# The linear attention's projections and decays first, two blocks' decays at once, softmax attention between its states

## The chip, the cores and the metric

The kernel runs on one core of a Trainium2 chip. The metric is device time in microseconds (us) for one launch. TensorE (PE in the profile) does the matrix products, VectorE (DVE) the elementwise and reducing work, ScalarE (ACT) the functions and most evictions of the matmul accumulators, GpSimd (POOL) and SyncE (SP) mostly issue transfers. Each engine executes its own list of instructions strictly in the order in which the program put them; an instruction that waits holds up everything behind it on its engine.

## What is computed

One decoder block for 512 tokens of width 1024, cut here to what matters:

```python
mod = silu(c) @ w_ada + b_ada                     # shift1, scale1, gate1, shift2, scale2, gate2
h = rms_norm(x, norm1_w) * (1 + scale1) + shift1
aq, ak, av, gq, gk, gv, gg, glr = split(h @ w_in)  # 512,128,128,256,256,512,512,16 columns
att = sliding_window_attention(aq, ak, av, sinks)  # 8 heads, 2 kv heads, window 128
log_a = log_sigmoid(glr @ gate_up + gate_bias) / 16
go = gla_chunked(gq, gk, gv, log_a)                # 4 heads: a decayed running state over the sequence
go = rms_norm(go, gla_norm_w) * silu(gg)
x = x + gate1 * (concat(att, go) @ w_out)
h2 = rms_norm(x, norm2_w) * (1 + scale2) + shift2
x = x + gate2 * peer_ffn(h2, wq, subkeys, u, v)    # product-key retrieval over 16384 experts
return rms_norm(x, final_norm_w)
```

In the linear attention, with b the running sum of log_a inside a block, the weight between a query at time t and a key at s <= t is sum over d of q[t,d] k[s,d] exp(b[t,d] - b[s,d]); the inner sum over earlier blocks is carried in a state S that is multiplied by exp(b_last) and gains k exp(b_last - b) times v.

## The kernel before

The tokens lie in four blocks of 128 (n = 0 to 3). The program has a **front**, all of the block up to the second norm, and then the expert part (queries against the keys, a dense product with u, routing, gathers). Only the front is touched by the change. Its steps:

- **mod_part(v)** makes one sixth of `mod` for all 1024 columns: the weights come as four 1 MB transfers (`wa`), and VectorE multiplies and adds eight 128x1024 slices into `macc` (L163, L165). Parts 0 and 1 are done in halves by `mod_half` (L228); `modT` (L234) then gives the scale and shift of the norm, and `h`, `hTh`, `hTl` (L257 to L261) are the normed, transposed tokens split into a high and a low part.
- **Projections.** `w_in` comes in nine groups of 256 columns, each a 1 MB transfer (`wi`). Groups 0 and 1 are the attention's queries, 2 its keys and values, 3 and 4 the linear attention's queries `gq` and keys `gk`, 5 and 6 its values `gv`, 7 and 8 its output gate `gg`. Each group is split into two halves of high and low parts (ScalarE L59, VectorE L60), and each product is three matmuls, high-high, low-high, high-low (L64 to L66). `proj_T` (groups 0 to 4) gives a transposed result in matmuls of 512 columns, `proj_N` (5 to 8) a plain one in matmuls of 256 columns.
- **attention(n)**: twice four heads: scores `sc` into the two-bank accumulator (L333), scaled and masked (L335), row maximum (L341), exponentials with row sums on ScalarE (L345), division (L351), transposes `pt` (L360) evicted by ScalarE to `PT` (L361), products with the values `po` (L366), eviction to `mixA` (L369).
- **decays**: `glr`, then `z`, `e`, and `la` (L375 to L394), from log_sigmoid.
- **gla_prep(n)**, for one block: the running sum `b` (L428), and for seven levels (halves of 64, 32, ..., 1 tokens) the difference to the middle of each group, the later half one way (L438), the earlier the other (L437), so that all exponents are negative; one exponential over all of E (L441); the late halves times q, the early halves times k (L445, L446).
- **gla_scores(n)**: matmuls of E with itself give each level's scores `pa` (L473, L478), in the same two-bank accumulator that the attention's scores use (one buffer), and VectorE copies each level's part into `at` under a mask (L481, L486).
- **gla_state(n)**: `go` from the state and from `at` (L496, L497), the state's update (L501 to L512), the norm of `go` into `gv` (L517 to L521).
- **gla_gate(n)**: gate times normed output (L526, L527), transposes `gt` (L530), high and low parts `gh`, `gl`, `ah`, `al` (L534 to L541).
- **mixers(n0)** for two blocks at a time: the product with `w_out` (`pw`, weights `wo`), `mg` and the residual `x` (L602, L603), the second norm `xn` (L611), transposes `x2t` (L620), `h` (L623), `h2Th`, `h2Tl` (L625, L626).

Weights that are to be split wait in a ring of three raw 1 MB buffers, shared by `wi` and `wa`; a transfer into a buffer starts when the last reader of its old content is done. The program's text gives the steps an order of importance; a scheduler turns it into the fixed list of each engine from its own estimate of the times, so a small change in the text moves instructions on all engines.

Order of the steps in the text before: projections 0, 1, 2; attention 0 to 3; decays; projection 3; mod 2; projection 4; masks; prep and scores 0; projections 5, 6; prep and scores 1; state 0; projection 7; mod 3; state 1; prep and scores 2; projection 8; mod 4; the silu of `gg`; gates 0 and 1; state 2; prep and scores 3; state 3; mixers of blocks 0, 1; gates 2 and 3; mixers of blocks 2, 3.

Of the kernel before, what the change touches and what calls it, by code (L numbers as in the profile page):

```python
# [41 lines left out]
def peer_block_kernel(ctx: ExitStack, tc: tile.TileContext, a: dict, out: bass.AP):  # L42
# [202 lines left out]
    for half in range(2):  # L245
        mod_half(1, half)
        if half == 1:
            fetch(a["w_in"][1], 1, 256, "wi")
        mod_half(0, half)
        if half == 0:  # L250
            fetch(a["w_in"][0], 0, 256, "wi")
        else:
            x_transposes(range(4, KD))
        for k in range(4 * half, 4 * half + 4):
# [6 lines left out]
            nc.vector.tensor_tensor(hTl[:, k, :], h32, hTh[:, k, :], OP.subtract)  # L261
# [39 lines left out]

    proj_T(0, (qT[:, 0, :], qT[:, 1, :]))
    proj_T(1, (qT[:, 2, :], qT[:, 3, :]), bank)
    vT = frA.tile([P, T], F32, tag="h32", bufs=4, name="vT")
    proj_T(2, (kT, vT))
    pv = bank("pv")
    for n in range(NT):
        nc.tensor.transpose(pv[:, n * P:(n + 1) * P], vT[:, n * P:(n + 1) * P], ident)
    nc.scalar.activation(vN.rearrange("p a b -> p (a b)"), pv, AF.Copy)


    am = frT.tile([P, 256], F32, name="am")
    nc.vector.memset(am, 0.0)
    nc.gpsimd.affine_select(am[:, :P], am[:, :P], pattern=[[1, P]], compare_op=OP.is_gt, fill=NEG,
                            base=0, channel_multiplier=-1)
    nc.gpsimd.affine_select(am[:, P:], am[:, P:], pattern=[[-1, P]], compare_op=OP.is_ge, fill=NEG,
                            base=0, channel_multiplier=1)
# [57 lines left out]
    wg = raw([P, KD, 16], "wglr")  # L375
    nc.sync.dma_start(wg, a["w_glr"])
    wgh, wgl = hilo(wg, [P, KD, 16], "wglr", nc.vector)
    pg = pbank("pglr")
    for k in range(KD):
        mm3(pg[:16, :], wgh[:, k, :], wgl[:, k, :], hTh[:, k, :], hTl[:, k, :], k == 0, k == KD - 1)  # L380
    nc.scalar.activation(glrT, pg[:16, :], AF.Copy)

    for j in range(2):
        pz = bank(f"pz{j}")
        nc.tensor.matmul(pz, gup[:, j * P:(j + 1) * P], glrT, start=True, stop=True)
        z = frA.tile([P, T], F32, tag="h32", bufs=4, name=f"z{j}")
        e = frA.tile([P, T], F32, tag="h32", bufs=4, name=f"e{j}")
        nc.scalar.activation(z, pz, AF.Identity, bias=gbT[:, j:j + 1])
        nc.scalar.activation(e, z, AF.Abs)
        nc.scalar.activation(e, e, AF.Exp, scale=-1.0)  # L390
        nc.scalar.activation(e, e, AF.Ln, bias=1.0)
        for n in range(NT):
            tsl = slice(n * P, (n + 1) * P)
            nc.vector.scalar_tensor_tensor(la[n][:, j, :], z[:, tsl], 0.0, e[:, tsl], op0=OP.min, op1=OP.subtract)  # L394
    proj_T(3, [[t[:, j, :] for t in gq] for j in range(2)])
    mod_part(2, frA, "m4", 2, dst=gate1b)
    proj_T(4, [[t[:, j, :] for t in gk] for j in range(2)])


    lm = frG.tile([P, NL + 1, P], BF, name="lm")  # L400
    ia = frA.tile([P, P], I32, tag="h32", bufs=4, name="ia")
    ib = frA.tile([P, P], I32, tag="h32", bufs=4, name="ib")
    nc.gpsimd.iota(ia, pattern=[[1, P]], base=0, channel_multiplier=0)
    nc.gpsimd.iota(ib, pattern=[[0, P]], base=0, channel_multiplier=1)
    xf = frA.tile([P, P], F32, name="xf")
    nc.vector.tensor_tensor(ia, ia, ib, OP.bitwise_xor)
    nc.vector.tensor_copy(xf, ia)
    nc.vector.tensor_scalar(lm[:, NL, :], iop, 0.0, None, op0=OP.is_gt)
    nc.vector.tensor_tensor(xf, xf, lm[:, NL, :], OP.mult)
    for L in range(NL):  # L410
        m = 64 >> L
        nc.vector.tensor_scalar(lm[:, L, :], xf, float(m), None, op0=OP.is_ge)
        nc.vector.scalar_tensor_tensor(lm[:, L, :], xf, float(2 * m), lm[:, L, :], op0=OP.is_lt, op1=OP.mult)
    nc.vector.tensor_copy(lm[:, NL, :], ident)
    sm = frG.tile([P, 256], F32, name="sm")
    nc.vector.memset(sm, 1.0)
    nc.vector.memset(sm.rearrange("p (a b) -> p a b", a=2)[:, :, 0:1], 0.0)
    S = [frG.tile([P, 2, P], F32, name=f"S{j}") for j in range(2)]
    for t in S:
        nc.gpsimd.memset(t, 0.0)  # L420

    def gla_prep(n, pool):
        b = pool.tile([P, 256], F32, tag="b", bufs=1, name=f"b{n}")
        q = pool.tile([P, 256], F32, tag="q", bufs=1, name=f"q{n}")
        k = pool.tile([P, 256], F32, tag="k", bufs=1, name=f"k{n}")
        v2 = lambda t: t.rearrange("p (j t) -> p j t", j=2)
        nc.vector.tensor_scalar(v2(b), la[n], 1.0 / TAU, None, op0=OP.mult)
        nc.vector.tensor_tensor_scan(b, sm, b, 0.0, op0=OP.mult, op1=OP.add)  # L428
        nc.vector.tensor_scalar(v2(q), gq[n], 0.125, None, op0=OP.mult)
        nc.vector.tensor_copy(v2(k), gk[n])  # L430
        E = pool.tile([P, NL + 2, 256], F32, tag="E", bufs=1, name=f"E{n}")
        half = lambda t, m: t.rearrange("p (g w) -> p g w", w=2 * m)
# [668 lines left out]
```

## Time and profile before

| what | value |
|---|---|
| time, median of 3 runs | 1595.04 us (1592.78 to 1595.13) |
| profiled execution | 1595.75 us, span 1594.0 us, mean granted TensorE clock 0.975 |
| TensorE / VectorE / ScalarE busy | 94% / 80% / 42% of the span |
| first matmul of the expert queries (`pq`), the end of the front | 319.03 us after the span's start |
| last matmul of the last projection (`pn`) | starts 190.15 us |
| last matmul with `w_out` (`pw`) | starts 291.76 us |

Rows of a timeline are: start (us), duration (us), engine, line, operation, result<-sources, shape, count, and in brackets how long the engine had been idle before it and whose event ended that wait. Rows of a group are: line, engine, operation, names, shapes, count | busy us, mean ns of one | idle us before them and its releasers. Rows of windows are: from:to, length, then for each engine the busy time (and the instructions), then the granted TensorE clock (1.00 is full), the transfer engines' share and GB/s. Durations in one engine's list can overlap a little: an instruction is fed while the one before it drains.

### The profile page before, as it was taken

How to read it: one execution, taken by the hardware profiler on the slowest of the kernel's cores; microseconds unless marked ns; L12 is line 12 of the kernel's file. 1: busy time of each engine (PE TensorE's matmuls, PEld its weight loads, DVE VectorE, ACT ScalarE, POOL GpSimd, SP SyncE). 2: the span in 40 equal slices, each digit the busy share in tenths (PEclk: the TensorE clock that was granted, in tenths of full speed). 3: DMA queues.
4: the chain of work that ended last, by engine and by line, in shares of the span. 5: the costliest groups of instructions: out<-in, count | busy, mean ns of one | idle time of the engine just before them, and what ended most of it. 6: DMA issues, size and time to landing. Idle time of an engine off the chain costs nothing.

```text
span 1594.0 us, 23349 instructions
## 1 busy us (share of the span) xinstructions
PE 1504.8 (94%) x8787; PEld 1339.3 (84%) x8787; DVE 1282.2 (80%) x2613; ACT 675.1 (42%) x1071; POOL 415.9 (26%) x323
## 2 busy tenths in 40 slices
PE   4999976699999999999899999999999999999997
PEld 3779865598898999999888888888888888888885
DVE  7587886459997899798578888878888788788987
ACT  5364533533344656665333333333333333333333
POOL 0000000034430000003233434434434444343550
PEclk9999978799999999999999999999999999999998
DMA  9525423335244767579988988989898998898893
GB/s 346 179 100 183 153 80 128 110 106 211 88 161 140 221 205 243 181 226 315 413 336 314 361 320 328 347 324 374 319 337 342 336 362 324 328 345 330 298 329 137
DMA packets 154928, 409.60 MB, mean 257 GB/s; under 512 B 10288, under 2 KB 77120, under 8 KB 142400
## 3 DMA queue, kind: packets, MB, share of 16 engines
q1 hardware_dynamic: 108736, 261.30, 46.5%
q0 software_dynamic: 36864, 134.23, 22.8%
q10 hardware_dynamic: 9216, 12.59, 2.1%
q8 instruction: 68, 1.11, 0.3%
q14 instruction: 44, 0.36, 0.1%
HBM read 366.14 MB, written 41.94 MB: 256 GB/s over the span
## 4 chain that ended last, share of the span: by engine, by line
PE 59%; DVE 5%; DMA 3%; ACT 1%; issue 1%; DVEq 0%; ACTq 0%
PE acc L65 11%; PE acc L64 11%; PE acc L66 11%; PE ph L66 8%; PE ph L64 8%; PE ph L65 8%; PE pg L824 3%; DVE o L817 1%; DMA u<-in_uT_dram 1%; DVE o L812 1%; DMA gr<-Gd 1%; DMA gu<-in_u_dram,ix_u 1%; ACT gs L826 0%; DVE oh L769 0%; DVE oh L767 0%
## 5 line engine op out<-in xcount | busy, mean ns | idle before, releaser
L837 POOL DMA_INDIRECT gu<-in_u_dram,ix_u x128 | 175.4, 1370 | 535.4 <-DVE o L817 275.2
L847 POOL DMA_INDIRECT gv<-in_vP_dram,ix_v x128 | 168.0, 1313 | 215.3 <-DVE gu L839 184.3
L852 DVE SCALAR_TENSOR_TENSOR gacc<-gv,hg,gacc 128x1024 f32<-128x1024 f32 x127 | 162.6, 1280 | 4.1 <-DMA gv<-in_vP_dram,ix_v 4.0
L839 DVE SCALAR_TENSOR_TENSOR gu<-gu,h2n 128x1024 f32<-128x1024 f32 x128 | 156.0, 1219 | 5.6 <-DMA gu<-in_u_dram,ix_u 5.6
L981 ACT ACTIVATE Ah<-ge 128x384 fp32r<-128x384 f32 x64 | 33.6, 525 | 155.5 <-PE acc L65 155.5
L981 ACT ACTIVATE Ah<-gel 128x384 fp32r<-128x384 f32 x64 | 33.6, 525 | 154.4 <-PE acc L65 154.4
L826 ACT ACTIVATE gs<-pg 128x512 f32<-128x512 f32 x96 | 94.3, 1104 | 9.9 <-PE pg L824 9.9
L817 DVE TENSOR_TENSOR o<-o,gp 128x1024 bf16<-128x1024 bf16 x144 | 91.0, 687 | 4.3
L824 PE MATMUL pg<-o,o 128*128 128x128 bf16 x1152 | 79.3, 223 | 5.8 <-DVE o L817 5.7
L824 PEld LDWEIGHTS <-o 128*128 128x128 bf16 x1152 | 69.3, 99 | 15.2 <-issue 8.4
L982 DVE TENSOR_TENSOR Al<-gel,Ah 128x384 fp32r<-128x384 f32 x64 | 35.6, 556 | 45.3 <-ACT Ah L981 45.3
L650 ACT ACTIVATE ge<-ph 128x384 f32<-128x384 f32 x128 | 60.7, 474 | 26.5 <-PE ph L66 26.4
L812 DVE TENSOR_TENSOR o<-iot,t 128x2048 bf16<-128x2048 bf16 x48 | 58.5, 1219 | 7.5 <-ACT t L792 7.5
L60 POOL TENSOR_TENSOR uc0l<-u,uc0h 128x1024 fp32r<-128x1024 f32 x1 | 2.8, 2838 | 197.4 <-ACT uc0h L59 197.4
L982 DVE TENSOR_TENSOR Al<-ge,Ah 128x384 fp32r<-128x384 f32 x64 | 35.5, 555 | 18.9 <-ACT Ah L981 18.7
L977 DVE TENSOR_TENSOR ge<-ge,gr 128x384 f32<-128x384 f32 x64 | 35.4, 553 | 13.5 <-ACT ge L650 13.5
L165 DVE SCALAR_TENSOR_TENSOR macc<-wa,scs,macc 128x1024 f32<-128x1024 f32 x28 | 39.9, 1425 | 6.6 <-DMA wa<-in_w_ada_dram 6.3
L977 DVE TENSOR_TENSOR gel<-gel,gr 128x384 f32<-128x384 f32 x64 | 32.8, 553 | 0.4 <-DMA gel<-gsp 0.4
L718 DVE MAX8 TVa<-scm 128x8 f32<-128x128 f32 x64 | 15.6, 306 | 18.8 <-ACT scm L710 18.8
L64 PE MATMUL pq<-h2Th,wq_0h 128*128 128x512 f32 (+1 forms) x80 | 29.4, 367 | 0.8 <-ACT h2n L633 0.8
L65 PE MATMUL pq<-h2Tl,wq_0h 128*128 128x512 f32 (+1 forms) x80 | 28.4, 355 | 0.0
L66 PE MATMUL pq<-h2Th,wq_0l 128*128 128x512 f32 (+1 forms) x80 | 28.3, 353 | 0.0
(2587 smaller groups left out, 5151.8 us busy)
## 6 DMA issues: line engine op xcount, KB each, us to landing
u<-in_uT_dram SPq DMA_DIRECT2D x64, 1024.0 KB, 8.4
v<-in_vP_dram SPq DMA_DIRECT2D x64, 1024.0 KB, 8.2
Gd<-gs SPq DMA_DIRECT2D x24, 1024.0 KB, 5.9
gr<-Gd SPq DMA_DIRECT2D x16, 1536.0 KB, 8.3
wa<-in_w_ada_dram SPq DMA_DIRECT2D x20, 1024.0 KB, 5.8
gsp<-ge ACTq DMA_DIRECT2D x64, 192.0 KB, 3.6
gel<-gsp SPq DMA_DIRECT2D x32, 384.0 KB, 6.5
wi<-in_w_in_dram SPq DMA_DIRECT2D x9, 1024.0 KB, 5.0
```

Source lines behind the costliest of these rows:

```text
L64: nc.tensor.matmul(acc, lh, rh, start=start, stop=False)
L65: nc.tensor.matmul(acc, lh, rl, start=False, stop=False)
L66: nc.tensor.matmul(acc, ll, rh, start=False, stop=stop)
L812: nc.vector.tensor_tensor(o12.rearrange("p g s k r -> p (g s) k r"), iot[:, None].to_broadcast([P, 2 * H, P, 2]), t12[:, g0:g0 + H].rearra ...
L817: nc.vector.tensor_tensor(o2[:, :, m], o12[:, :, 1], gp3[:, g0:g0 + H, m, None].to_broadcast([P, H, P, 2]), OP.mult)
L824: nc.tensor.matmul(pt[:, i, :], o12[:, g, 0, :, r], o2[:, g, m, :, r], start=(m == 0), stop=(m == 2))
L826: nc.scalar.activation(gs[:, :, t0 + 4 * f:t0 + 4 * f + 4].rearrange("p b a -> p a b"), pt, AF.Copy)
L837: nc.gpsimd.indirect_dma_start(out=ur, out_offset=None, in_=a["u"], in_offset=bass.IndirectOffsetOnAxis(ap=ix_u[:, s:s + 1], axis=0))
L839: nc.vector.scalar_tensor_tensor(ur, ur, 1.0, h2n, op0=OP.mult, op1=OP.mult, accum_out=hid[:, s:s + 1])
L847: nc.gpsimd.indirect_dma_start(out=vr, out_offset=None, in_=a["vP"], in_offset=bass.IndirectOffsetOnAxis(ap=ix_v[:, s:s + 1], axis=0))
L852: nc.vector.scalar_tensor_tensor(gacc, vr, hg[:, s:s + 1], gacc, op0=OP.mult, op1=OP.add)
L982: nc.vector.tensor_tensor(Al, gef, Ah, OP.subtract)
```

## The change

Only the front changes, in these ways.

1. **Order of the text**: projection 3, decays, projection 4, projection 0, mod 2, prep of blocks 0 and 1, projection 1, scores 0, projection 2, attention 0, scores 1, projection 5, attention 1, prep of blocks 2 and 3, projection 6, state 0, attention 2, scores 2, state 1, projection 7, attention 3, scores 3, projection 8, silu, state 2, state 3, mod 3, mod 4, then gates 0 to 3, mixers of blocks 0, 1, mixers of blocks 2, 3. The groups fetched ahead are 3 and 4, not 0 and 1.
2. **Prep for two blocks at once**, 512 columns wide: one subtraction a level (all with the same sign), then the absolute value on ScalarE and one exponential with the scale -1/16. The division by 16 and the factor 0.125 of `gq` move into that scale and into the eviction of projection 3; the copies of `q` and `k` go away.
3. **One E for both preps**, which later holds the gate: `gg[n]` is the n-th slice of E. The evictions of projections 7 and 8 therefore come after the reads of E by scores 2 and 3.
4. **Gate**: `gg` is multiplied by the norm weight for all blocks after the silu; blocks 2 and 3 take the gate in the instruction that norms `go`. `ah` is made in one instruction instead of two, `al` too.
5. Masks, states and the eight `at` tiles (four before) are set up at the very start; `wg` has buffers of its own; the pool `gp` of the expert part is allocated later.

The scheduler's lists show where this puts the instructions. Three places follow.

**VectorE around the norm's end**, where `hTl`, the low part of the normed tokens, is made (names: `macc_308`/`macc_355` the last half part of mod 1 or 0, `macc_1056`/`macc_650` the sums of mod 2, `wa_0`, `wa_2` its 1 MB pieces). Before:

```order
L228 SCALAR_TENSOR_TENSOR macc_308<-mixA_126,scs,macc_308 128x512
L234 TENSOR_TENSOR modT<-mt,vec 128x4
L259 TENSOR_SCALAR h_7_358<-xt_341,aT,modT 128x512
L261 TENSOR_TENSOR hTl<-h_4_346,hTh 128x512
L261 TENSOR_TENSOR hTl<-h_7_358,hTh 128x512
```

After:

```order
L267 SCALAR_TENSOR_TENSOR macc_355<-mixA_117,scs,macc_355 128x512
L202 TENSOR_SCALAR macc_650<-wa_0_651,scs 128x1024
L204 SCALAR_TENSOR_TENSOR macc_650<-wa_0_651,scs,macc_650 128x1024
L273 TENSOR_TENSOR modT<-mt,vec 128x4
L298 TENSOR_SCALAR h_7_405<-xt_388,aT,modT 128x512
L204 SCALAR_TENSOR_TENSOR macc_650<-wa_2_655,scs,macc_650 128x1024 x2
L300 TENSOR_TENSOR hTl<-h_4_393,hTh 128x512
L300 TENSOR_TENSOR hTl<-h_7_405,hTh 128x512
```

Four instructions of mod 2 now stand ahead of `hTl`.

**TensorE in the attention's middle** (`sc` scores, `pt` transposes, `po` products with values, `pj` and `pn` projections, `mt` the column sums of mod 3 and 4, `gb` those of mod 2). Before, with projection matmuls above and below:

```order
L66 MATMUL pj_1027<-hTh,wi_1l 128x512
L333 MATMUL sc_688<-kT,qT 128x256 x3
L366 MATMUL po_562<-PT_589,vN 64x128 x4
L360 MATMUL pt_627<-ident,sS_600 128x128 x4
L333 MATMUL sc_688<-kT,qT 128x256
L172 MATMUL gb_1075<-macc_1056,ones 128x512
L366 MATMUL po_562<-PT_626,vN 64x128 x4
L333 MATMUL sc_738<-kT,qT 128x256 x4
L64 MATMUL pj_1091<-hTh,wi_0h 128x512
```

After, from the last matmul of projection 6 (the next projection matmul, of projection 7, stands 30 rows further on):

```order
L66 MATMUL pn_1681<-wi_1h,hTl 128x256
L384 MATMUL sc_1190<-kT,qT 128x256 x4
L384 MATMUL sc_1425<-kT,qT 128x256 x4
L216 MATMUL mt_2096<-ones,macc_2079 128x1 x8
L411 MATMUL pt_1168<-ident,sS_1141 128x128 x4
L417 MATMUL po_1140<-PT_1167,vN 64x128 x4
L411 MATMUL pt_1179<-ident,sS_1141 128x128 x4
L417 MATMUL po_1140<-PT_1178,vN 64x128 x4
L411 MATMUL pt_1216<-ident,sS_1189 128x128 x4
L384 MATMUL sc_1473<-kT,qT 128x256 x4
```

In the 30 rows between projections 6 and 7 there are attention 1 and 2, scores 2, state 0 and the column sums, and no projection.

**VectorE in that same stretch** has the sums of mod 4 (`macc_2106`) between the attention's steps:

```order
L204 SCALAR_TENSOR_TENSOR macc_2106<-wa_2_2111,scs,macc_2106 128x1024
L402 TENSOR_SCALAR sS_1189<-sS_1189,Z_1198 128x256 x4
L204 SCALAR_TENSOR_TENSOR macc_2106<-wa_2_2111,scs,macc_2106 128x1024
L386 SCALAR_TENSOR_TENSOR sS_1424<-sc_1425,am 128x1024
L204 SCALAR_TENSOR_TENSOR macc_2106<-wa_4_2115,scs,macc_2106 128x1024
L392 TENSOR_REDUCE mx_1431<-sS_1424 128x4
```

Before, these sums stood among the projections' and the later states' instructions. The diff, cut to its core (mod_part, mixers and the expert part keep their text):

```diff
-    for n in range(NT):
+    for i in range(2):
         for nm, lst in (("la", la), ("gq", gq), ("gk", gk)):
-            lst.append(frG.tile([P, 2, P], F32, tag="blk", bufs=3 * NT, name=f"{nm}{n}"))
+            lst.append(frG.tile([P, 2, 2, P], F32, tag="blk", bufs=6, name=f"{nm}{i}"))
-    gg = [frG.tile([P, 512], F32, tag="gg", bufs=NT, name=f"gg{n}") for n in range(NT)]
+    Eg = frG.tile([P, NL + 2, 512], F32, name="Eg")
+    gg = [Eg[:, n, :] for n in range(NT)]
...
-            fetch(a["w_in"][1], 1, 256, "wi")
+            fetch(a["w_in"][4], 4, 256, "wi")
...
-            fetch(a["w_in"][0], 0, 256, "wi")
+            fetch(a["w_in"][3], 3, 256, "wi")
...
-    for n in range(NT):
-        attention(n)
...
+    def gla_prep(i):
+        flat = lambda t: t.rearrange("p n j t -> p (n j t)")
+        q, k = flat(gq[i]), flat(gk[i])
+        b = frG.tile([P, 512], F32, tag="b", bufs=1, name=f"b{i}")
+        for n in range(2):
+            c2 = slice(n * 256, (n + 1) * 256)
+            nc.vector.tensor_tensor_scan(b[:, c2], sm, flat(la[i])[:, c2], 0.0, op0=OP.mult, op1=OP.add)
+        E = Eg
...
         for L in range(NL):
             m = 64 >> L
-            bv, ev = half(b, m), half(E[:, L, :], m)
-            ref = bv[:, :, m - 1:m].to_broadcast([P, 128 // m, m])
-            nc.vector.tensor_tensor(ev[:, :, :m], ref, bv[:, :, :m], OP.subtract)
-            nc.vector.tensor_tensor(ev[:, :, m:], bv[:, :, m:], ref, OP.subtract)
...
+            bv = grp(b, 2 * m)
+            nc.vector.tensor_tensor(grp(E[:, L, :], 2 * m), bv, bv[:, :, m - 1:m].to_broadcast([P, 256 // m, 2 * m]),
+                                    OP.subtract)
...
-        nc.scalar.activation(E, E, AF.Exp)
...
+        nc.scalar.activation(E[:, :NL, :], E[:, :NL, :], AF.Abs)
+        nc.scalar.activation(E[:, :NL + 1, :], E[:, :NL + 1, :], AF.Exp, scale=-1.0 / TAU)
+        nc.scalar.activation(E[:, NL + 1, :], b, AF.Exp, scale=1.0 / TAU)
...
+            if gated:
+                nc.vector.scalar_tensor_tensor(gv[n][:, gsl], go[:, gsl], r4[:, h:h + 1], gg[n][:, gsl], op0=OP.mult,
+                                               op1=OP.mult)
+            else:
+                nc.vector.tensor_scalar(gv[n][:, gsl], go[:, gsl], r4[:, h:h + 1], None, op0=OP.mult)
...
+    proj_T(3, [[t[:, :, j, :] for t in gq] for j in range(2)], scale=0.125)
+    decays()
+    proj_T(4, [[t[:, :, j, :] for t in gk] for j in range(2)], bank)
+    proj_T(0, (qT[:, 0, :], qT[:, 1, :]))
+    mod_part(2, frA, "m4", 2, dst=gate1b)
+    gla_prep(0)
+    proj_T(1, (qT[:, 2, :], qT[:, 3, :]), bank)
+    gla_scores(0)
...
+    attention(0)
+    gla_scores(1)
     proj_N(5, gv, 0)
+    attention(1)
+    gla_prep(1)
     proj_N(6, gv, 256)
-    gla_ahead(1)
-    gla_state(0, *ats[0])
+    gla_state(0, False)
+    attention(2)
+    gla_scores(2)
+    gla_state(1, False)
     proj_N(7, gg, 0)
-    mod_part(3, frA, "m4", 2)
-    gla_state(1, *ats[1])
-    gla_ahead(2)
+    attention(3)
+    gla_scores(3)
     proj_N(8, gg, 256)
-    mod_part(4, frA, "m4", 2)
     for t in gg:
         nc.scalar.activation(t, t, AF.Silu)
...
+    gla_state(2, True)
+    gla_state(3, True)
+    mod_part(3, frA, "m4", 2)
+    mod_part(4, frA, "m4", 2)
...
-    for n in (0, 1):
+    for n in range(NT):
         gla_gate(n)
-    gla_state(2, *ats[2])
-    gla_ahead(3)
-    gla_state(3, *ats[3])
-    mixers(0)
-    for n in (2, 3):
-        gla_gate(n)
-    mixers(2)
+    for n in range(0, NT, 2):
+        mixers(n)
```

More of the change, by code (lines that the diff above doesn't have):

```diff
@@ L147, in peer_block_kernel @@
     gup = frA.tile([16, 256], F32, name="gup")
+    am = frT.tile([P, 256], F32, name="am")
+    nc.vector.memset(am, 0.0)
+    nc.gpsimd.affine_select(am[:, :P], am[:, :P], pattern=[[1, P]], compare_op=OP.is_gt, fill=NEG,
+                            base=0, channel_multiplier=-1)
+    nc.gpsimd.affine_select(am[:, P:], am[:, P:], pattern=[[-1, P]], compare_op=OP.is_ge, fill=NEG,
+                            base=0, channel_multiplier=1)
+    lm = frG.tile([P, NL + 1, P], BF, name="lm")
+    ia = frA.tile([P, P], I32, tag="h32", bufs=4, name="ia")
+    ib = frA.tile([P, P], I32, tag="h32", bufs=4, name="ib")
+    nc.gpsimd.iota(ia, pattern=[[1, P]], base=0, channel_multiplier=0)
+    nc.gpsimd.iota(ib, pattern=[[0, P]], base=0, channel_multiplier=1)
+    xf = frA.tile([P, P], F32, name="xf")
+    nc.vector.tensor_tensor(ia, ia, ib, OP.bitwise_xor)
+    nc.vector.tensor_copy(xf, ia)
+    nc.vector.tensor_scalar(lm[:, NL, :], iop, 0.0, None, op0=OP.is_gt)
+    nc.vector.tensor_tensor(xf, xf, lm[:, NL, :], OP.mult)
+    for L in range(NL):
+        m = 64 >> L
+        nc.vector.tensor_scalar(lm[:, L, :], xf, float(m), None, op0=OP.is_ge)
+        nc.vector.scalar_tensor_tensor(lm[:, L, :], xf, float(2 * m), lm[:, L, :], op0=OP.is_lt, op1=OP.mult)
+    nc.vector.tensor_copy(lm[:, NL, :], ident)
+    sm = frG.tile([P, 256], F32, name="sm")
+    nc.vector.memset(sm, 1.0)
+    nc.vector.memset(sm.rearrange("p (a b) -> p a b", a=2)[:, :, 0:1], 0.0)
+    S = [frG.tile([P, 2, P], F32, name=f"S{j}") for j in range(2)]
+    for t in S:
+        nc.gpsimd.memset(t, 0.0)
+    atz = [frG.tile([P, 2, P], F32, name=f"at{i}") for i in range(8)]
+    for t in atz:
+        nc.gpsimd.memset(t, 0.0)
     nc.scalar.activation(scs, cT, AF.Exp, scale=-1.0)
@@ L300, in proj_N, with decays @@
                 nc.scalar.activation(dst[n + s][:, col:col + 256], pt[:, s, :], AF.Copy)
[L302 to L317, printed above, removed]
+    def decays():
+        pg = pbank("pglr")
+        for k in range(KD):
+            mm3(pg[:16, :], wgh[:, k, :], wgl[:, k, :], hTh[:, k, :], hTl[:, k, :], k == 0, k == KD - 1)
+        nc.scalar.activation(glrT, pg[:16, :], AF.Copy)
+        for j in range(2):
+            pz = bank(f"pz{j}", ("pt", "po")[j])
+            nc.tensor.matmul(pz, gup[:, j * P:(j + 1) * P], glrT, start=True, stop=True)
+            z = frA.tile([P, T], F32, tag="h32", bufs=4, name=f"z{j}")
+            e = frA.tile([P, T], F32, tag="h32", bufs=4, name=f"e{j}")
+            nc.scalar.activation(z, pz, AF.Identity, bias=gbT[:, j:j + 1])
+            nc.scalar.activation(e, z, AF.Abs)
+            nc.scalar.activation(e, e, AF.Exp, scale=-1.0)
+            nc.scalar.activation(e, e, AF.Ln, bias=1.0)
+            for i in range(2):
+                tsl = slice(i * 256, (i + 1) * 256)
+                two = lambda t: t[:, tsl].rearrange("p (n t) -> p n t", n=2)
+                nc.vector.scalar_tensor_tensor(la[i][:, :, j, :], two(z), 0.0, two(e), op0=OP.min, op1=OP.subtract)
     def attention(n):
@@ L369, in attention @@
         nc.scalar.activation(mixA[n].rearrange("p a b -> p (a b)"), po, AF.Copy)
-    for n in range(NT):
-        attention(n)
[L375 to L432, printed above, removed]
+    def gla_prep(i):
[6 more added lines that the diff above has]
+        E = Eg
+        grp = lambda t, w: t.rearrange("p (g w) -> p g w", w=w)
@@ L462, in gla_scores @@
+    preps = {}
+    def gla_scores(n):
+        q, k, E = preps[n // 2][:3]
+        off = n % 2 * 256
         U16 = mybir.dt.uint16
@@ L495, in gla_state @@
             if n > 0:
-                nc.tensor.matmul(go[:, gsl], qe[:, j * P:(j + 1) * P], S[j][:, s, :], start=True, stop=False)
+                nc.tensor.matmul(go[:, gsl], qe[:, off + j * P:off + (j + 1) * P], S[j][:, s, :], start=True, stop=False)
             nc.tensor.matmul(go[:, gsl], at[j][:, s], gv[n][:, gsl], start=(n == 0), stop=True)
@@ L867, in peer_block_kernel @@
     gather_to.n = 0
-    for n in (0, 1):
+    for n in range(NT):
         gla_gate(n)
-    gla_state(2, *ats[2])
-    gla_ahead(3)
-    gla_state(3, *ats[3])
-    mixers(0)
-    for n in (2, 3):
-        gla_gate(n)
-    mixers(2)
+    for n in range(0, NT, 2):
+        mixers(n)
     frW_s.close()
```

92 lines of the change are left out of this document (49 added, 43 removed).

## The prediction

> **What bounds the kernel now.** I read the engines' shares first, then windows over the front, then the gaps in TensorE's timeline.
>
> ```profile
> span 1594.0 us, 23349 instructions
> PE 1504.8 (94%) x8787; PEld 1339.3 (84%) x8787; DVE 1282.2 (80%) x2613; ACT 675.1 (42%) x1071; POOL 415.9 (26%) x323
> ```
>
> Over the span TensorE is the bound, but that average is made by the expert part, which the change leaves as it is: from the first matmul of the expert queries (`pq`, 319.03 us) every engine has the same rows in the same order. So the question is when `pq` starts. The windows show the front, columns busy us of PE, PEld, DVE, ACT, POOL, then the granted TensorE clock:
>
> ```profile
> 100.00:150.00 50.00, 48.72 (x369) 42.87 (x366) 41.85 (x110) 25.69 (x71) 0.00 (x0) 1.00 0.34 117
> 200.00:250.00 50.00, 38.84 (x245) 31.64 (x245) 44.89 (x143) 19.23 (x37) 0.00 (x0) 0.80 0.33 103
> 250.00:300.00 50.00, 32.44 (x164) 24.73 (x164) 31.90 (x69) 22.02 (x48) 2.84 (x1) 0.81 0.36 130
> ```
>
> In the middle TensorE is 97% busy at full clock, since projection matmuls stand between the steps of attention and states. After 200 us the projections are used up: of 100 us TensorE is busy 71, and part of that at a lower clock.
>
> ```profile
> 190.15 0.28 PE L66 MATMUL pn<-wi_1h,hTl 128*128 128x256 f32 x1
> ...
> 205.81 0.79 PE L496 MATMUL go<-S,qe 128*128 128x128 f32 x2 [5.36 <-DVE gv L521]
> ...
> 291.76 0.40 PE L66 MATMUL pw<-wo2142h,gl 128*128 128x512 f32 x1
> 298.67 1.11 PE L620 MATMUL x2t<-ident,xn 128*128 128x128 f32 x4 [6.51 <-DVE xn L611]
> ...
> 319.03 0.58 PE L64 MATMUL pq<-h2Th,wq_0h 128*128 128x256 f32 x1 [0.78 <-ACT h2n L633]
> ```
>
> From the last projection to the last `pw` are 101.7 us, and then 26.9 us of second norm. Call the end of the last projection X: before, X = 190.4 and `pq` follows 128.6 us later. The change shortens what comes after X and makes X later. Both have to be priced.
>
> **What the change removes: the late states.** States 2 and 3, scores 2 and 3, and their waits leave the stretch behind X or stand ready there. After X the list of TensorE has 192 matmuls of 512 columns with `w_out`, the four gates' transposes, the two last state products, and `x2t` of two blocks. Matmuls of 512 columns follow each other at 0.2267 us on average, those of 256 at 0.1267 (the pair below, and the last `pn` above, which starts 0.12 after this one):
>
> ```profile
> 50.60 0.39 PE L65 MATMUL pj<-hTl,wi_1h 128*128 128x512 f32 x1
> 50.83 0.39 PE L66 MATMUL pj<-hTh,wi_1l 128*128 128x512 f32 x1
> ...
> 190.03 0.28 PE L65 MATMUL pn<-wi_1l,hTh 128*128 128x256 f32 x1
> ```
>
> 192 x 0.2267 = 43.5, and some 54 small ones of about 0.15 (four `pt` take 0.65, in a row below) give 8.1: 51.6 us, where before 101.7 passed. I take it without gaps, because behind X each operand is made while `pw` runs. Then comes the norm chain. Before it takes 26.9 us; in the new list block 1's norm and `h2Tl` stand behind the split of two weight pieces, and the residual load of block 3 is issued later. I add 4 us for that (none and 8 are the bounds; nothing before shows it): 31. Behind X it is thus 82.6 us, 46 less than before. **If X came as before the kernel would gain 46 us.**
>
> **What it adds at the start.** Four sums of mod 2 stand ahead of `hTl`, which gates the low-part matmuls of the first projections.
>
> ```profile
> 43.60 1.22 DVE L60 TENSOR_TENSOR wi_1l<-wi,wi_1h 128x1024 fp32r<-128x1024 f32 x1
> 44.73 0.75 DVE L228 SCALAR_TENSOR_TENSOR macc<-mixA,scs,macc 128x512 f32<-128x512 f32 x1
> 46.62 0.16 DVE L234 TENSOR_TENSOR modT<-mt,vec 128x4 f32<-128x4 f32 x1 [1.15 <-PE mt L232]
> 49.55 2.50 DVE L261 TENSOR_TENSOR hTl<-h,hTh 128x512 fp32r<-128x512 f32 x4 [1.92 <-ACT hTh L260]
> ...
> 66.12 0.75 DVE L163 TENSOR_SCALAR macc<-wa,scs 128x1024 f32<-128x1024 f32 x1 [4.94 <-DMA wa<-in_w_ada_dram]
> ```
>
> ```profile
> wa<-in_w_ada_dram SPq DMA_DIRECT2D x20, 1024.0 KB, 5.8
> ```
>
> The second piece can load only when a raw buffer is free, at 44.8 us, when the split at 43.60 has ended; 5.5 us later it lands, at 50.3; two sums of 1.2 us follow, and `hTl` starts at 52.7 instead of 49.55. TensorE's L65 moves from 50.60 to 53.45: **+2.9 us**, and queued behind it are all low-part products, so nothing hides it.
>
> **What it moves: the middle.** After that start TensorE has dense work until the first `pa`. Of projections 3, 4, 0, 1 and 2 (48 matmuls of 0.2267 each, 54.4 us) and of `glr` (5.4) some 50 high-part matmuls are done before; 48 us remain, with about 3 us for the first prep: 104.5 us. From here VectorE decides. Its groups:
>
> ```profile
> L165 DVE SCALAR_TENSOR_TENSOR macc<-wa,scs,macc 128x1024 f32<-128x1024 f32 x21 | 26.9, 1280 | 5.6 <-DMA wa<-in_w_ada_dram 5.5
> L163 DVE TENSOR_SCALAR macc<-wa,scs 128x1024 f32<-128x1024 f32 x3 | 2.3, 754 | 6.4 <-DMA wa<-in_w_ada_dram 6.4
> L481 DVE COPY_PREDICATED at<-lm,pa 128x128 f32<-128x128 uint16 x56 | 18.8, 336 | 1.5 <-PE pa L478 0.6
> L60 DVE TENSOR_TENSOR wi_1l<-wi,wi_1h 128x1024 fp32r<-128x1024 f32 x9 | 11.0, 1219 | 6.1 <-ACT wi_1h L59 6.1
> L445 DVE TENSOR_TENSOR E<-E,q 128x128 f32<-128x128 f32 x28 | 7.6, 288 | 0.5 <-ACT E L441 0.5
> L335 DVE SCALAR_TENSOR_TENSOR sS<-sc,am 128x1024 f32<-128x1024 f32 x6 | 7.3, 1218 | 4.5 <-PE pt L360 4.5
> L341 DVE TENSOR_REDUCE mx<-sS 128x4 f32<-128x1024 f32 x6 | 7.3, 1214 | 0.0
> L351 DVE TENSOR_SCALAR sS<-sS,Z 128x256 f32<-128x256 f32 x24 | 6.8, 347 | 0.1
> L451 DVE TENSOR_TENSOR qe<-E,q 128x256 f32<-128x256 f32 x4 | 1.7, 419 | 0.0
> ```
>
> Neighbours overlap by about 0.08 us (four `hTl` of 0.684 mean take 2.50), so I sum distances: 1.2 for 1024 columns, 0.6 for 512, 0.335 for 256. From the copies of the first `pa` to the last instruction ahead of attention 1 VectorE has 28 level copies and 8 narrower ones (11.8), five weight splits (6.1), attention 0 (6.6), five sums of mod 3 (5.9), seven subtractions (4.8) and `al` (0.7): 36 us, and 8 us of waits, since `pa` and `sc` share one accumulator and each waits for the last reader of the other: 148.5.
>
> From there to the last copy of scores 2 it has four L335 and four L341 (9.3), 16 L351 (4.2), ten sums and a first one (13.0), fourteen level products of 256 columns (4.7), 18 copies (5.9), eight state updates (2.2), the norms of `go` and two `al` (2.5), the rest small: **47.5 us**, to 196. TensorE has in that stretch no projection, only pieces like these, 16 us in all:
>
> ```profile
> 117.65 0.66 PE L366 MATMUL po<-PT,vN 128*64 128x128 f32 x8
> 118.24 0.65 PE L360 MATMUL pt<-ident,sS 128*128 128x128 f32 x4
> 187.75 0.95 PE L473 MATMUL pa<-E 64*128 64x64 f32 x14
> ```
>
> Seven such `po`, eight `pt`, two `pa` with their L478, the scores, state 0 and the column sums; so TensorE idles about 30 us here. Projections 7 and 8 cannot fill it, because they evict into E, which scores 2 and 3 still read. They follow with 24.3 us (192 x 0.1267), with attention 3, scores 3 and state 1 between them (9): 33 us, starting when `pa` of scores 2 is written, about 3 us before the last copy. X = 196 - 3 + 33, and about 4 for `pt` waiting behind copies: **230**.
>
> Three costs come on top. *Sums waiting for transfers*: a raw buffer is held by the last weight group through the whole stretch, so mod 3 and 4 go through two; before, 12 us of such waits (L163 and L165) stand ahead of 24 sums, half of which lie here: 5 us (0 if other VectorE work always fits, 12 if all of it comes here). *Handing over between engines* in attention's chain: 3 us (0 to 6; L335 shows 4.5 of waits for six). *The clock*:
>
> ```profile
> 206.00:212.00 6.00, 2.79 (x12) 2.50 (x13) 5.96 (x24) 0.63 (x1) 0.00 (x0) 0.50 0.00 0
> 218.00:224.00 6.00, 6.00 (x36) 5.15 (x35) 5.24 (x18) 1.25 (x4) 0.00 (x0) 0.56 0.09 31
> 270.00:280.00 10.00, 3.35 (x12) 2.38 (x13) 5.83 (x18) 5.80 (x18) 0.00 (x0) 0.56 0.00 0
> ```
>
> A stretch where TensorE is a third busy had 0.56 of the clock, and a wholly busy one after a gap still had 0.56 for 6 us. At half clock the 16 us become up to 32, mostly behind VectorE; I take 4 us (0 to 10) of it and the restart as visible. Together X = 242, bounds 230 to 258; `pq` = 242 + 82.6 = 324.6, **+5.6 us**.
>
> The rule of the Trainium skill, "TensorE: Matmul & The Clock Gate", section "Part 1: The HAM clock gate", is that one idle window of about 3.4 us throttles the array to 4/8 and about 3.4 us of sustained work releases it. The rows above agree on the half, not on the release, which took longer here; by the rule an estimate of the restart's price is 1.7 us in place of about 4, and the sum would come out near 1599.
>
> **What is cheaper in itself.** A pair's prep costs VectorE about 12 us, two single ones 16; this is in the sums above. ScalarE has more work (the absolute value, from `E` below about 3.3 us a pair, and a wider exponential), in the shade of VectorE except once, before the first `pa`, where the 3 us stand.
>
> ```profile
> L441 ACT ACTIVATE E<-E 128x2304 f32<-128x2304 f32 x4 | 8.5, 2128 | 2.2 <-DVE E L440 2.2
> ```
>
> The masks set up early fall into VectorE's idle time before 33 us, and `gp`'s later allocation touches nothing in the front: nothing for both, at most 2 us if the masks delay the first sums.
>
> **The rivals.** *A, the forecast*: X between 234 and 252. Against the profiled 1595.75 it is 1595.75 + 5.6 = 1601.4, and the median lies 0.7 below that run: 1600.6, 1601 rounded. *B, faster*: the stretch between projections 6 and 7 runs with few waits, because VectorE always has something ready, and the clock holds. For it: 206 to 212 us before had VectorE full (5.96 of 6), and the sums are in the list as filler. Then X = 215 to 233, and with X = 222 the time is 1601 - 20 = 1581. Against it: attention's chain goes through three engines four times in that stretch. *C, clearly slower*: the clock stays at half until projection 7 is well under way, and the projections, 24.3 us, run half their length at it (+12), beside full transfer waits. X = 255 to 262; time 1614 to 1621, deciding from about 8 us of half clock behind the restart on. For it: the 6 us at 0.56 above; against it: dense work after 224 us had the full clock. *D, nothing happens*: X falls at 237 by chance and the two moves cancel, about 1595.7; it is the lower end of A and of "same".
>
> **How the numbers follow.** Chances: A 0.46, B 0.36, C 0.18. What a measurement of this kernel can tell from no change is about 0.2%, 3.2 us: from X 233 to 240 it is "the same". Faster: B and little else, 0.36. Same: the lower part of A, 0.19. Slower: the upper part of A, 0.27, and C, 0.18: 0.45. A alone gives 1593 to 1611; the range takes in B down to X = 215 and the near half of C, 1574 to 1614.
>
> **What would show it.** Right: `hTl` about 3 us later; TensorE in long gaps with VectorE over 85% busy between the last matmul of projection 6 and the first of projection 7, granted clock there near 0.5; last `pn` near 242; behind it `pw` nearly without gaps for some 52 us; last `pw` to `pq` near 31 us. Wrong: the last `pn` before 230 (B), or `pw` with gaps as before, so that the 46 us behind X are not gained, or a `pq` at the same place whose followers run differently.

## The result and the profile after

The changed kernel takes 1613.2 us (median of 4 runs, 1611.94 to 1614.96) where the kernel before takes 1594.75: a ratio of 1.0119, 95% interval 1.0101 to 1.0137. It is slower by 1.2%; the profiled execution spans 1610.2 us, 16.2 more than before.

The page's totals, and four windows over the front (columns busy us of PE, PEld, DVE, ACT, POOL, granted clock, transfers' share, GB/s), in the changed kernel:

```profile
span 1610.2 us, 23258 instructions
PE 1519.0 (94%) x8787; PEld 1351.9 (84%) x8787; DVE 1277.2 (79%) x2509; ACT 680.9 (42%) x1061; POOL 412.1 (26%) x327
```

```profile
100.00:150.00 50.00, 45.24 (x421) 40.90 (x421) 37.02 (x89) 19.33 (x41) 0.00 (x0) 0.97 0.24 84
150.00:200.00 50.00, 37.12 (x210) 29.30 (x206) 41.91 (x97) 18.54 (x57) 0.00 (x0) 0.60 0.44 150
200.00:250.00 50.00, 46.90 (x368) 40.57 (x369) 24.84 (x72) 18.57 (x51) 0.00 (x0) 0.74 0.07 22
250.00:300.00 50.00, 49.39 (x256) 40.74 (x255) 37.32 (x64) 30.69 (x60) 0.00 (x0) 1.00 0.62 205
```

The kernel before, from 150 to 200 us:

```profile
150.00:200.00 50.00, 47.83 (x464) 43.15 (x464) 43.25 (x116) 24.59 (x52) 0.00 (x0) 1.00 0.55 178
```

The poor stretch has moved. Before, TensorE was dense and at full clock until 200 us and thin behind; now it is thin at 0.60 of the clock from 150 to 200, busy but at 0.74 of the clock until 250, and dense at full clock behind. The marks on TensorE's timeline:

```profile
53.06 0.50 PE L65 MATMUL pj<-hTl,wi_1h 128*128 128x512 f32 x1 [0.31 <-DVE hTl L300]
...
251.66 0.28 PE L66 MATMUL pn<-wi_1h,hTl 128*128 128x256 f32 x1
...
304.36 0.40 PE L66 MATMUL pw<-wo2142h,gl 128*128 128x512 f32 x1
319.63 1.09 PE L642 MATMUL x2t<-ident,xn 128*128 128x128 f32 x4 [9.58 <-DVE xn L633]
...
339.23 0.58 PE L64 MATMUL pq<-h2Th,wq_0h 128*128 128x256 f32 x1 [0.69 <-ACT h2n L655]
```

The last projection ends at X = 251.9 (190.4 before), `pw` takes 52.8 us behind it (101.7 before), the second norm 34.5 (26.9 before), and `pq` comes 20.2 us later. The part behind `pq` is 4 us shorter than before (1271.0 against 1275.0). It varied between 1269.6 and 1274.8 us in the other kernels whose later part is the same, so no cause is given for it.

### The profile page after: what moved, and what is told of

Its sections match the earlier page's. It is cut to its first block, busy times and chain, and to the rows that moved or that the text cites. A ratio compares the mean times of both kernels' runs of the same rounds, so it can differ in the third digit from the quotient of the medians.

```text
span 1610.2 us, 23258 instructions
## 1 busy us (share of the span) xinstructions
PE 1519.0 (94%) x8787; PEld 1351.9 (84%) x8787; DVE 1277.2 (79%) x2509; ACT 680.9 (42%) x1061; POOL 412.1 (26%) x327
## 3 DMA queue, kind: packets, MB, share of 16 engines
q8 instruction: 69, 1.13, 0.3%
## 4 chain that ended last, share of the span: by engine, by line
PE 61%; DVE 3%; DMA 2%; ACT 1%; issue 1%; DVEq 0%; ACTq 0%; SPq 0%
PE acc L65 11%; PE acc L64 11%; PE acc L66 11%; PE ph L66 8%; PE ph L64 8%; PE ph L65 8%; PE pg L846 4%; DMA Gd<-gs 1%; DMA gr<-Gd 1%; DVE o L839 0%; ACT gs L848 0%; DVE oh L791 0%; DVE o L834 0%; DVE oh L789 0%; DMA u<-in_uT_dram 0%
## 5 line engine op out<-in xcount | busy, mean ns | idle before, releaser
L859 POOL DMA_INDIRECT gu<-in_u_dram,ix_u x128 | 170.3, 1330 | 532.9 <-DVE o L839 272.8
L482 DVE COPY_PREDICATED at<-lm,pa 128x128 f32<-128x128 uint16 x56 | 19.0, 340 | 15.4 <-PE pa L479 14.1
L65 PE MATMUL pq<-h2Tl,wq_0h 128*128 128x512 f32 (+1 forms) x80 | 28.5, 356 | 0.0
```

What stands on the lines that cost most here:

```text
L65: nc.tensor.matmul(acc, lh, rl, start=False, stop=False)
L859: nc.gpsimd.indirect_dma_start(out=ur, out_offset=None, in_=a["u"], in_offset=bass.IndirectOffsetOnAxis(ap=ix_u[:, s:s + 1], axis=0))
```

## The experiments

Each kernel was compared with the kernel before on the same chip. "Copies of scores 2" are the last masked copies of that step, the end of the stretch that the prediction called the middle; where two kernels are compared, the time is the start of their last row (it takes 0.6 us). Times of single runs are marked as such.

### The gate out of E

```diff
-    gg = [Eg[:, n, :] for n in range(NT)]
...
+    gg = [frG.tile([P, 512], F32, tag="blk", bufs=6, name=f"gg{n}") for n in range(NT)]
     proj_N(7, gg, 0)
```

> The gate no longer lies in E: its four tiles take the place of la, gq and gk of the first blocks, which are free by then, so projections 7 and 8 can be evicted while scores 2 and 3 still read E. Theory 1 (the shared E shuts the projections out of the attention's middle, and TensorE idles at half clock there): the last pn falls from 251.8 us to 220 to 235, the granted clock from 148 to 202 us rises from 0.59 to over 0.9, the time falls from 1613 to 1588 to 1600. Rival (VectorE's chain sets the end whatever TensorE does): the last pn stays within 5 us of 251.8 and the time at 1608 to 1614.

Measured: 1597.3 us, ratio 1.0034 (1.0021 to 1.0047), so 0.85% or some 14 us come back. The window from 148 to 202 us, first of the changed kernel, then of this one:

```profile
148.00:202.00 54.00, 39.61 (x226) 31.47 (x226) 44.81 (x103) 20.98 (x60) 0.00 (x0) 0.59 0.44 153
```

```profile
148.00:202.00 54.00, 47.02 (x346) 41.34 (x346) 43.61 (x79) 33.23 (x74) 0.00 (x0) 0.81 0.51 172
```

The projections do fill the middle: 346 matmuls in place of 226, and the last one starts at 180.6 us, far earlier than the 220 to 235 that was expected. The clock rises to 0.81, not to the 0.9 that was expected. But `pq` only moves from 339.2 to 325.2, since attention 2 and 3 and scores 2 and 3 now go on behind the last projection. The theory holds for the 14 us. For the rest the rival is right that filling TensorE does not shorten the chain: the copies of scores 2 come at 219.0 us, later than the 212.2 of the changed kernel.

### TensorE filled with work that nobody uses

```diff
                         h, l, k == 0, k == KD - 1)
+                if g == 7 and n == 2 and s == 0:
+                    for i in range(160):
+                        nc.tensor.matmul(pt[:, 1, :P], ident, gv[3][:, :P], start=True, stop=True)
```

> 160 matmuls of 128x128 whose results nobody uses stand between the two halves of projection 7 and fill TensorE's idle time in the attention's middle. They do no useful work and take about 0.15 us each at half clock. Theory 2 (half clock is a large part of what the middle costs): granted clock from 148 to 202 us over 0.85 instead of 0.59, the last copy of scores 2 comes at 200 to 206 instead of 212.8 us, the last pn 5 to 12 us earlier, the time 1602 to 1609. Rival (the clock is hidden behind VectorE, the price is handing over between engines): the clock rises, the last copy of scores 2 stays within 3 us or comes later, the time is 1610 to 1622.

```profile
148.00:202.00 54.00, 52.60 (x472) 48.18 (x474) 44.67 (x100) 21.12 (x61) 0.00 (x0) 0.97 0.46 154
```

```profile
207.54 0.61 DVE L491 COPY_PREDICATED at<-lm,pa 64x128 f32<-64x128 uint16 x2
```

The clock is back, 0.97 for 0.59, and the copies of scores 2 come 4.7 us earlier (207.54 against 212.22). The time is 1617.2, ratio 1.0162 (1.0139 to 1.0185). An added matmul took 0.23 us at full clock, more than the 0.15 that was expected, so the last 24 of them (5.7 us) ran behind the copies, and the scheduler now put the column sums of mod 3 and 4 there too (3.9 us); together they cost more than the clock gives. So the clock's share inside the stretch is about 5 us, less than expected, and what it costs behind it is not shown by this run.

### The same with narrow matmuls

```diff
-                        nc.tensor.matmul(pt[:, 1, :P], ident, gv[3][:, :P], start=True, stop=True)
+                        nc.tensor.matmul(pt[:64, 1, :64], ident[:64, :64], gv[3][:64, :64], start=True, stop=True)
```

with 360 in place of 160.

> As the filled stretch, but the unused matmuls are narrow: 360 of 64 rows by 64 columns instead of 160 of 128 by 128. Theory (what keeps or returns the granted clock is how much of the array works, not whether TensorE has an instruction: from 202 to 214 us the changed kernel's TensorE was busy without a gap, mostly with narrow matmuls, at 0.50): TensorE busy over 45 of 54 us from 148 to 202, and the granted clock there still below 0.70. Rival (any unbroken run of matmuls brings the clock back): 0.85 or more, as with the wide ones (0.97).

```profile
148.00:202.00 54.00, 51.70 (x658) 45.72 (x660) 45.39 (x102) 22.25 (x62) 0.00 (x0) 0.94 0.48 157
```

The theory falls as far as it speaks of keeping the clock: narrow matmuls hold it nearly as well as wide ones (0.94 for 0.97). Whether they return it is not shown, since the full clock was there at 155.3 us, before the first of them ran at 158.1. The time, 1623.3 us (one run), is longer still; 120 of the narrow matmuls ran by themselves from 213.0 to 227.2 us, 14.2 us.

### Without the sums of parts 3 and 4

```diff
-    mod_part(3, frA, "m4", 2)
-    mod_part(4, frA, "m4", 2)
+    nc.gpsimd.memset(modT[:, 24:40], 0.0)
+    nc.vector.scalar_tensor_tensor(aT[:, 1, :], modT[:, 32:40], 1.0, n2T, op0=OP.add, op1=OP.mult)
```

> Parts 3 and 4 of the modulation are left out (shift 0 and scale 1 for the second norm): 16 sums of VectorE, 8 MB of transfers and 16 small matmuls less in the attention's middle. Theory 3 (the sums and their transfers take VectorE's time there: some 15 us of work and 5 of waiting): the last pn falls by 10 to 18 us, the time to 1595 to 1603. Rival (they only fill waits): the last pn falls by less than 5 us, the time stays above 1608.

Measured: 1587.9 us (one run), 0.9974 of the kernel before on the same chip, so some 23 us less than the changed kernel. The copies of scores 2 come at 190.5 us, 21.8 earlier, and the last `pn` starts at 229.2, 22.5 earlier, more than the 10 to 18 that were expected. The 16 sums are 1 x 0.74 + 7 x 1.28 twice, 19.4 us, and 4.6 us of waits for their transfers stand ahead of them in VectorE's timeline (0.88, 1.84, 0.55, 0.94 and 0.35): together 24. X moves by what VectorE had to do, almost one for one. They did not fill waits; VectorE's work sets most of the middle's length. The run also took the column sums out of TensorE's list, and the clock from 148 to 202 us rose to 0.87; how much of the 22 us is theirs is not shown.

### The sums early

```diff
+    def mod_early(v):
...
+            acc = (vN.rearrange("p a b -> p (a b)"), kT)[half]
+            tiles = [t for t in gv] + [t.rearrange("p a b -> p (a b)") for t in mixA]
...
     mod_part(2, frA, "m4", 2, dst=gate1b)
+    for v in (3, 4):
+        mod_early(v)
     gla_prep(0)
```

> Parts 3 and 4 of the modulation are computed in full, but from weights that load into the tiles of gv and mixA (free until projection 5 and attention 0), so VectorE can do the 32 half-width sums before 110 us, where it was busy 29 of 50 us. All else as in the changed kernel. Theory (VectorE's work between 126 and 200 us sets the end of the middle): the last pn falls from 251.7 us by 15 to 22, as where the sums were left out (229.2), the time to 1590 to 1600. Rival (the sums and 8 MB of transfers now delay the norm and the first projections by as much): the first copies of scores 0 end at 120 us or later instead of 110.5, and the time stays above 1605.

Measured: 1603.1 us, ratio 1.0058 (1.0041 to 1.0075): some 10 us come back, less than half of the 23, and the time lies between the two forecasts. The first copies of scores 0 come to their last row at 120.1 us instead of 110.5, so the rival takes its 9.6 us, and the theory the rest: X falls by 10.7, to a last `pn` at 241.0.

### Both

> Both edits together: early sums, and the gate in the freed tiles of la, gq and gk. Theory (two separate costs, 14 us for the gate in E and some 20 for the sums' place): 1572 to 1583 us, faster than the kernel before (1592 on this chip's last comparison). Rival (both remove the same wait, the chain of attention 1 to 3 on VectorE): 1587 to 1598.

Measured: 1588.4 us, ratio 0.9963 (0.9948 to 0.9977), faster than the kernel before. Against the changed kernel that is 1.56%; the two edits alone gave 0.85% and 0.61%, 1.46% together. They are separate costs, as the theory says; its 1572 to 1583 was missed because the early sums alone bring 10 us and not 20. The time lies in the rival's range, but not for the rival's reason.

### The chain of the second norm

```diff
-            x1s.append(frW.tile([P, D], F32, tag="x1", bufs=2, name=f"x1_{n}"))
+            x1s.append(frW.tile([P, D], F32, tag="x1", bufs=4, name=f"x1_{n}"))
```

> The residual tiles x1 of the mixers get four buffers instead of two, so that the loads for blocks 2 and 3 do not wait until blocks 0 and 1 are through the second norm. Theory 4 (the late residual load makes the norm chain 34.6 us long from the last pw to pq, 26.9 in the kernel before): the chain falls to 26 to 30 us, the time to 1605 to 1609. Rival (the order of VectorE's instructions makes the chain long, not the load): the chain stays at 33 to 36 us and the time within 2 us of 1613.

Measured: 1610.9 us, ratio 1.0109 (1.0087 to 1.0131), which the changed kernel's interval overlaps, and 35.2 us from the end of the last `pw` to `pq`. The late residual load alone is not the cause. The second try gives the norm's own tiles a second buffer:

```diff
-        xn2 = frW.tile([P, D], F32, tag="xn2", bufs=1, name=f"xn2_{n}")
+        xn2 = frW.tile([P, D], F32, tag="xn2", bufs=2, name=f"xn2_{n}")
...
-        h32 = frW.tile([P, KD, P], F32, tag="h2_32", bufs=1, name=f"h2_{n}")
+        h32 = frW.tile([P, KD, P], F32, tag="h2_32", bufs=2, name=f"h2_{n}")
```

(with three residual tiles, and two buffers for the norm's squares, which share `h2_32`).

> The changed kernel with two buffers for the second norm's xn2 and h2_32 and three for the residual, so that block 1's norm need not be finished in the same tiles before blocks 2 and 3 begin. Theory (three norms in a row on single tiles, of blocks 1, 2 and 3, lie behind the last pw, where the kernel before has two; the late residual load alone is not it, since four residual tiles left the chain at 35.6 us): the chain from the last pw to pq falls from 34.9 to 25 to 29 us, the time by 5 to 9 us, to 1604 to 1608. Rival (the chain is set by ScalarE's own work): it stays above 32 us.

```profile
301.68 0.47 PE L66 MATMUL pw<-wo2142h,gl 128*128 128x512 f32 x1
...
329.98 0.58 PE L64 MATMUL pq<-h2Th,wq_0h 128*128 128x256 f32 x1 [0.69 <-ACT h2n L655]
```

The chain falls from 34.5 to 27.8 us, the time to 1607.2, ratio 1.0086 (1.0070 to 1.0101, which just touches the changed kernel's interval). For the chain the theory holds: with one buffer block 1's norm, too, lay behind the last `pw` (its `xn` starts at 306.6 us in the changed kernel, and here at 295.2, before it). Whether the third residual tile has a part in the 6.7 us was not tried by itself. On top of the two earlier edits the same one gave nothing that can be measured:

> The three edits together: early sums, gate in the freed tiles, two buffers for the second norm. Theory (three separate costs that add): 4 to 8 us below the kernel with the first two (1588), 1580 to 1585, ratio to the kernel before 0.990 to 0.994. Rival (the norm chain is hidden again by TensorE's pw, which ends later): no change, ratio 0.995 to 0.998.

Measured: 1587.9 us, ratio 0.9962 (0.9948 to 0.9976). There `pq` comes 3.4 us earlier (311.25 against 314.67), and the part behind it is 3 us longer; why is open.

### The new arithmetic in the old order

This kernel keeps the prep for two blocks, the single subtraction, the fused gate and the early masks, but writes the steps in the order of the kernel before; the gate lies in the freed tiles.

> The new arithmetic (prep of two blocks at once, one subtraction a level, fused gate, masks at the start) in the order of the kernel before: projections 0, 1, 2, attention 0 to 3, decays, projections 3 and 4, and so on, with the late states 2 and 3 and scores 3 between the gates and the mixers. The gate lies in the freed tiles. Theory (the arithmetic saves VectorE some 7 to 16 us, part of it in the stretch behind the projections; the order is what costs): 1580 to 1593 us. Rival (the wider prep and E used by both pairs cost as much as the order): above 1600.

Measured: 1608.6 us, ratio 1.0089 (1.0073 to 1.0106). This could have passed for a verdict on the arithmetic, but the window from 100 to 150 us says otherwise:

```profile
100.00:150.00 50.00, 35.08 (x186) 21.70 (x187) 25.91 (x65) 23.81 (x68) 0.00 (x0) 0.73 0.06 21
```

TensorE is idle for 30% and VectorE for half of that stretch: the changed kernel takes the decays' two accumulators from the attention's banks, so in the old order the decays and all that comes behind them wait for the attention's end. One argument was put back to what the kernel before has:

```diff
-            pz = bank(f"pz{j}", ("pt", "po")[j])
+            pz = bank(f"pz{j}")
```

> As the new arithmetic in the old order, but the decays' two accumulators come from the pair of banks that the kernel before used, not from those of the attention's transposes and products. In the first try the decays and projection 3 waited behind the attention, and TensorE was busy 35 of 50 us from 100 to 150. Theory (with that wait gone the new arithmetic is no loss in the old order): 1583 to 1596 us. Rival (E for a pair, one buffer, makes the second pair's prep wait for scores 1 and costs whatever the order): 1600 or more.

```profile
100.00:150.00 50.00, 46.65 (x336) 37.39 (x336) 43.58 (x90) 31.80 (x68) 0.00 (x0) 0.97 0.32 105
...
200.00:250.00 50.00, 48.92 (x374) 42.03 (x374) 45.63 (x102) 29.51 (x50) 0.00 (x0) 1.00 0.38 124
```

Measured: 1580.6 us, ratio 0.9913 (0.9897 to 0.9929). The arithmetic is worth 0.9%, 14 us, and the stretch behind 200 us, poor before, is dense. Between this kernel and the changed one lie 2.1%, 33 us: 14 of them are the gate in E, as measured in the new order, and the other 19 the order, with the accumulators that go with it. With the norm's second buffers:

> The new arithmetic in the old order (decays' banks as before, gate in the freed tiles) with two buffers for the second norm and three residual tiles. Theory (the chain behind the last pw, 31.8 us there, is set by the norms that wait for single tiles, and adds to the rest): the chain falls to 25 to 29 us, the time from 1580.6 to 1574 to 1578, ratio to the kernel before 0.986 to 0.990. Rival (in this order block 1's norm is done before the last pw anyway, and the chain is that of two norms): no change, 1579 to 1583.

```profile
274.51 0.40 PE L66 MATMUL pw<-wo2142h,gl 128*128 128x512 f32 x1
...
302.95 0.58 PE L64 MATMUL pq<-h2Th,wq_0h 128*128 128x256 f32 x1 [0.69 <-ACT h2n L650]
```

Measured: 1576.9 us, ratio 0.9899 (0.9879 to 0.9919), the fastest of all. The chain is 28.0 us instead of 31.4; as for the time, the two intervals overlap, so the last 4 us are likely but not shown.

## Why the prediction was right, and by how much not

It said slower, by 5.6 us on the profiled execution, with 1574 to 1614 as the range and a chance of 0.45 for slower. The direction and the mechanism were right and the time lies inside, close to the upper end: 1613.2 is above the 1611 that the prediction's own case, A, reached up to. The size, 16.2, was three times the forecast. By its steps:

- **The late states leave the stretch behind X: right.** `pw` and its companions took 52.8 us without a gap of note; 51.6 were forecast.
- **The start: right.** L65 came at 53.06 (53.45 forecast), 2.5 us later than before, behind two sums that waited for a transfer:

```profile
49.80 2.60 DVE L204 SCALAR_TENSOR_TENSOR macc<-wa,scs,macc 128x1024 f32<-128x1024 f32 x2 [1.79 <-DMA wa<-in_w_ada_dram]
52.33 2.49 DVE L300 TENSOR_TENSOR hTl<-h,hTh 128x512 fp32r<-128x512 f32 x4
```

- **VectorE decides the middle: right in the main**, as leaving out the sums shows. Its length came out right, but partly by luck. From attention 1's first instruction to the end of the last copy of scores 2 it took 59.3 us, 47.5 of work and 12 of waits, hops and clock having been forecast:

```profile
153.49 1.23 DVE L386 SCALAR_TENSOR_TENSOR sS<-sc,am 128x1024 f32<-128x1024 f32 x1
...
209.59 2.59 DVE L482 COPY_PREDICATED at<-lm,pa 128x128 f32<-128x128 uint16 x7 [8.53 <-PE pa L479]
212.22 0.61 DVE L487 COPY_PREDICATED at<-lm,pa 64x128 f32<-64x128 uint16 x2
```

VectorE worked for 43.0 of them, 72% and not the over 85% that was named as a sign, and stood idle for 16.3. More than half of that is one wait at the end, 8.5 us for `pa`, while TensorE was busy at half clock; in the filled stretch the same wait was 4.7. TensorE was idle for 13 us of the 59, not for some 30.
- **The start of the middle: 5 us off.** It began at 153.5, not 148.5. VectorE's first copies came at 107.0, not 104.5, and from there it took 46.5 us and not 44. The scores `sc` waited for the copies and ran at half clock (2.08 us, where 1.13 was usual), but that is not what attention 1 waited for: they were done at 151.5, and VectorE was on a sum and a weight split until 153.5.

```profile
149.39 2.08 PE L384 MATMUL sc<-kT,qT 64*128 64x256 f32 x8 [4.49 <-DVE at L487]
```

```profile
151.04 1.29 DVE L204 SCALAR_TENSOR_TENSOR macc<-wa,scs,macc 128x1024 f32<-128x1024 f32 x1 [0.55 <-DMA wa<-in_w_ada_dram]
152.24 1.22 DVE L60 TENSOR_TENSOR wi_0l<-wi,wi_0h 128x1024 fp32r<-128x1024 f32 x1
```

- **Projections 7 and 8 behind it: mis-sized, in ways that partly cancel.** The prediction, and the text on the change ahead of it, took the 30 rows without a projection to lie between projections 6 and 7. They lie within 7: 48 of its 96 matmuls stand ahead of them, and only the second halves, whose accumulators wait for evictions into E (the first two run at 203.8 and 204.7 us), stand behind. So 144 matmuls followed, 18.2 us at the forecast's distance, not 24.3. But from the end of the last copies to X passed 39.1 us where 34 were forecast. TensorE restarted at half clock, and a second fall came with scores 3:

```profile
202.00:214.00 12.00, 12.00 (x78) 0.50 0.01 1
214.00:216.00 2.00, 2.00 (x14) 0.68 0.00 0
216.00:218.00 2.00, 2.00 (x20) 1.00 0.00 0
```

```profile
212.80:251.90 39.10, 36.12 (x300) 31.95 (x299) 22.36 (x62) 17.06 (x47) 0.00 (x0) 0.84 0.12 38
```

Of the 39.1 us TensorE was idle for 3.0 and busy for 36.1 at a mean clock of 0.84, so about 6 of them are the price of the half clock. The 134 projection matmuls in it make 17 at the forecast's distance, so some 13 are left for the small matmuls of attention 3, scores 3 and state 1, for which 9 were priced. This is worked out from these rows and not tested by a run of its own. The half clock that goes on behind the restart is rival C's mechanism, though X stayed below the 255 to 262 of C. The forecast gave 4 us for the clock in all; the filled stretch shows about 5 inside the middle, and these rows some 6 behind it. X came at 251.9, the upper end of A, instead of 242.
- **The norm chain: mis-sized.** 4 us were added to 26.9 for "block 1's norm and the late residual load"; 7.6 came. Block 1's norm is the cause (two buffers, with a third residual tile, removed 6.7); the residual load, named beside it, is not the cause by itself (four tiles removed nothing).
- **The clock gate's rule** (the Trainium skill, "TensorE: Matmul & The Clock Gate", "Part 1: The HAM clock gate": about 3.4 us of sustained work releases the clock) would have made the restart's term smaller, 1.7 us by the estimate in the prediction. The rows above disagree: 12 us without an idle moment in the records stayed at 0.50.
- **Rival B** (full waits covered by sums) is refuted by the copies of scores 2 at 212 us and by X, **rival D** by 1.2%.

The sum: X +9.9 against the forecast, `pw` +1.2, chain +3.5, so `pq` at 339.2 and not 324.6; the part behind it 4 us shorter.

What the prediction did not ask is what the new arithmetic would do in the old order. It priced VectorE's gain at 4 us a pair and let it vanish in the sums; there it was worth 14 us.

## What to carry to other kernels

Matmuls that wait for nothing are what covers a chain through three engines, so look where an order uses them up, and whether a shared buffer (here E, for the gate) shuts the remaining ones out just where they are needed. Where one engine has work without a due time in such a chain (the sums), take it out once: if the end moves by as much as that engine had to do, its work is on the path there, whatever its mean share says. And before an experiment that undoes one part is read, look at its own profile for a wait that it made itself, as the decays' banks did.
